# A decoder layer in fp32: convolution and later additions issued inside the next unit of products, whole results added up by one transfer, fewer operand sums by transfer, buffer halves paired by group

## The chip, the cores and the metric

The kernel runs on one core of a Trainium2 chip. The metric is device time in microseconds, from the first to the last instruction of the core and what lies around it. Three runs of the kernel before took 2989.66, 2991.01 and 2994.32 us; the median, 2991.01 us, is the time before. Engines are named as the profile names them: PE multiplies matrices, DVE works on vectors, ACT evaluates functions and copies with a scale, POOL issues transfers here (and does little else), SP issues loads.

## The reference

One decoder layer on 512 tokens with 2048 features, in fp32. The first half is a mixer (two kinds of attention, with a projection in and out); the change touches only where it stores some of its results. The second half is where most of the change lies:

```python
def conv_ffn(h, w_up, conv_w, conv_b, w_down):
    u = h @ w_up                                  # 512 x 2048 times 2048 x 11264
    S = u.shape[1]
    up = jnp.pad(u, ((0, 0), (CONV_WIDTH - 1, 0), (0, 0)))
    u = conv_b + sum(conv_w[i] * up[:, i:i + S] for i in range(CONV_WIDTH))
    a, b = jnp.split(u, 2, axis=-1)
    return (jax.nn.silu(a) * b) @ w_down          # 512 x 5632 times 5632 x 2048

def reference(x, c, positions, ...):
    ...
        h = rmsnorm(x, g_ffn[layer]) * (1 + sc2) + sh2
        x = x + (1 + gt2) * conv_ffn(h, w_up[layer], conv_w[layer], conv_b[layer], w_down[layer])
    return rmsnorm(x, g_final)
```

## The kernel before, in words

Features lie on the 128 partitions and the 512 tokens along the free axis. Each fp32 operand is split into a rounded high part and the rest: `parts` makes `wh` on ACT (L140) and `wl` on DVE (L142) of a weight chunk of 128x1024, and there are three buffers for each of the two. A product is then a few matmuls with high and low parts.

Most of the large products are done in **units** (`unit`). A unit computes two 128x512 results, `c1` and `c2`, from four quarters of a weight matrix (A11, A12, A21, A22, each 128x1024) with seven products instead of eight. In PE's order these are B11, T1, T2, B21, T3, B22 and T4. They take as weights a11; s = a21 + a22; s + a11; a12; a11 + a21; a12 + s; a22. Their outputs go to three banks, r1, r2 and r3. B21 adds onto r1 after B11 has been read from it, T3 and then T4 add onto r2 after what stands there was read, and B22 adds onto r3 after T1 was read. So PE waits for ACT's and DVE's readings of the banks as well as for its weights. Consecutive units take turns with two sets of banks, "acc" and "att".

In a **wide** unit the moving operand of six products has 512 columns: high and low part of the other factor side by side. Each bank then holds two 256-column partial results, which have to be summed, and part of these additions is done by transfers that add to their destination (`add`, L242, issued by POOL). Such a unit issues four of 128 KB: `l1` onto the left half of c1, `p5` onto the right half of c2, `u2` onto the right half of c1, and at the end `p1` onto the left half of c2. `l1` and `u2` are halves of a tile "sp", `p1` and `p5` are halves of a tile "ta". Two stages use wide units: 41 for `w_up` and 8 for `w_down1`. The units of `w_up` also make two of the weight sums by transfer (`by_dma`): s is a21 with a22 added from memory, and d = a21 + a11 is a second load of a21 with a11 added from memory.

After a unit of `w_up` comes `finish`: for each of the two results a causal convolution (`conv`: one pass of ACT, L1039, and two of DVE, L1040 and L1041), a Silu on ACT (L1046), a multiplication on DVE (L1048) and a store (L1049). The results of three further blocks, `ups`, come from a plain product ahead of the units and are finished beside the first three units. After a unit of `w_down1` each result is added to an earlier partial sum that a transfer loads (L1145, L1146), and stored (L1147).

Weights come through a ring of eight buffers "raw", loaded by SP in program order. Results and split operands lie in 31 tiles "F" of 128x1024; `slot` hands out halves of such a tile, two consecutive requests of the same group sharing one, and a tile comes free when both halves are done with.

The program is written as one sequence; a scheduler sets the order of each engine's instructions when it is built. Each engine then works through its own list strictly in order, and an instruction that waits holds up everything behind it on that engine. `behind(pins)` makes the scheduler issue what stands inside it only after the pinned instructions. `unit` has two such places: `between(0, ...)` after the copy of T1's result, and `between(1, ...)` after the copies of B21's result.

Of the kernel before, what the change touches and what calls it, by code (L numbers as in the profile page):

```python
# [35 lines left out]
NU = 3  # L36
# [39 lines left out]
def block_kernel(ctx: ExitStack, tc: tile.TileContext, A: dict, out: bass.AP):  # L76
# [151 lines left out]
    def unit(src, f, between=lambda *_: None, wide=False, by_dma=False):  # L228
# [27 lines left out]
        if by_dma:  # L256
            s = a21
            add(s, src[3])
        else:
            a22 = load(src[3], w)  # L260
        a12 = load(src[1], w)
        if by_dma:
            d = load(src[2], w)
            add(d, src[0])
            a22 = load(src[3], w)
        product(r1, parts(a11, w), "B11", True)
        e = t2k("ta", 2)
        p1, p5 = both(e)
# [5 lines left out]
        if not by_dma:  # L274
            s = t2k("raw", 8, w=w)
            last_v = tt(s, a21, a22, ALU.add)
# [6 lines left out]
        u2, l1 = both(e)  # L283
# [7 lines left out]
        if wide:  # L291
            last = act(l1, r1[:, HALF:], AF.Copy)
            add(c1[:, :HALF], l1)
# [7 lines left out]
        if wide:  # L301
            tt(c2[:, HALF:], r2[:, HALF:], c2[:, HALF:], ALU.add)
            add(c2[:, HALF:], p5)
        else:
            tt(c2[:, HALF:], c2[:, HALF:], p5, ALU.add)
        tt(a12, a12, s, ALU.add)  # L306
        product(r3, parts(a12, w), "B22", False)
        if wide:
            act(c1[:, HALF:], r3[:, :HALF], AF.Copy)
            tt(u2, r3[:, HALF:], u2, ALU.add)  # L310
            add(c1[:, HALF:], u2)
        else:
            tt(c1[:, HALF:], r3[:, :HALF], u2, ALU.add)
        product(r2, parts(a22, w), "T4", False)
        if wide:
            act(c2[:, :HALF], r2[:, :HALF], AF.Copy)
            tt(p1, r2[:, HALF:], p1, ALU.subtract)
            add(c2[:, :HALF], p1)
        else:
            tt(c2[:, :HALF], r2[:, :HALF], p1, ALU.subtract)  # L320
# [118 lines left out]
    def evac(ps, rows=slice(0, P)):  # L439
        o = slot()  # L440
        act(o[rows], ps[rows], AF.Copy)
        return o
# [232 lines left out]
    def fetch(src, rows=slice(0, P)):  # L675
        t = slot()
        save(t[rows], src[rows])
        return t
# [7 lines left out]
    def values(g, vs):  # L686
# [12 lines left out]
        for b in range(NQB):  # L699
            vs.append(evac(pv[b]))  # L700
# [11 lines left out]
    def indexer():  # L712
# [11 lines left out]
        bias.extend(slot()[:, : (b + 1) * P] for b in range(1, NQB))  # L724
# [65 lines left out]
    pairs = [[fetch(xd[2 * i]), fetch(xd[2 * i + 1])] for i in range(1)]  # L790
# [49 lines left out]
    def stick_4(hd, w, vs):  # L840
# [4 lines left out]
        ya[hd] = evac(o)  # L845
# [7 lines left out]
    va = [fetch(vd[b]) for b in range(NQB)]  # L853
    before = None
    def turned(hd):
        pair = [fetch(xd[16 + 2 * hd + i]) for i in range(2)]
        for t in pair:
            rope(t, [t], cosT, sinT, 64)
        return pair

    td = dram("td", KT)
    for hd in range(NH):
        state = stick_1(hd)
        if hd + 1 < NH:
            pairs.append([fetch(xd[2 * hd + 2]), fetch(xd[2 * hd + 3])])
        if before:
            stick_4(*before, va)
            if hd % 4 == 0:
                va = [fetch(vd[hd + b]) for b in range(NQB)]
        run(fill, 1 if hd < 4 else 2)  # L870
        if hd == NH - 1:
            cosT, sinT = (fetch(rope_d[0][:, i * S : (i + 1) * S]) for i in range(2))
            for i in range(4):
                ya[i] = fetch(yad[i])
# [51 lines left out]
    def sparse_4(hd, pT, vs, y):  # L926
# [5 lines left out]
        y.append(evac(o))  # L932

    def branch_a():
        w = prep(A["w_a"][0])
        g = fetch(xd[32])
        for j in range(KT):
            ahead = (prep(A["w_a"][j + 1]), fetch(xd[34 + 2 * j])) if j + 1 < KT else (None, None)
# [37 lines left out]
    for j in range(KT):  # L976
        t = t2k("w", 2)
        save(t, td[j])
        g = fetch(xd[33 + 2 * j])
# [314 lines left out]
```

## Time and profile before

| what | value |
|---|---|
| median of three runs | 2991.01 us |
| the profiled execution | 2988.76 us |
| its span, first to last instruction | 2986.8 us |
| PE busy in the span | 2814.4 us, 94% |
| DVE busy | 2343.7 us, 78% |
| ACT busy | 1420.4 us, 48% |
| POOL busy | 509.9 us, 17% |
| granted PE clock, mean | 0.982 |
| bytes moved by transfers | 598.41 MB, 200 GB/s |

A busy PE is not PE at its peak, because matmuls overlap; what counts is how long PE waits and how far apart matmuls start. Idle time of an engine that nothing waits for costs nothing. The stage of the `w_up` units runs from about 1528 to 2497 us, that of `w_down1` from about 2560 to 2722 us.

### The profile page before, as it was taken

The numbers are of one execution on the slowest core, as the hardware profiler recorded it, in microseconds if no ns is written. First come the engines' busy times: TensorE is split into PE (matmuls) and PEld (weight loads), VectorE is DVE, ScalarE is ACT, GpSimd is POOL, SyncE is SP. The second block draws the span as 40 slices with busy tenths as digits, with TensorE's granted clock in tenths as the row PEclk, the third lists the DMA queues.
The fourth block names the chain that finished last, engine by engine and source line by source line (L and its number), as shares of the span: only waits on it lengthen the run. The fifth ranks groups of instructions, "written<-read, shape, count | busy, mean of one in ns | idle before, by whom it ended". The sixth has DMA issues, their size and how long they took to land.

```text
span 2986.8 us, 45295 instructions
## 1 busy us (share of the span) xinstructions
PE 2814.4 (94%) x17174; PEld 2484.2 (83%) x17174; DVE 2343.7 (78%) x3448; ACT 1420.4 (48%) x2083; POOL 509.9 (17%) x727
## 2 busy tenths in 40 slices
PE   7999999999999999999998888889889899998998
PEld 6779999999987778899887777777777778887887
DVE  8979888888877998899877676766667777887555
ACT  5554544455546555344554444444444445544222
POOL 0000000100111211112212222222222221221111
PEclk9999999999999999999999999999999999999999
DMA  9954456555563668644467888777878786668754
GB/s 350 339 205 157 151 198 208 194 166 183 191 239 129 221 202 285 228 163 163 170 167 181 198 191 189 186 187 192 196 188 192 192 194 221 186 174 268 245 185 141
DMA packets 196186, 598.41 MB, mean 200 GB/s; under 512 B 24368, under 2 KB 53936, under 8 KB 195968
## 3 DMA queue, kind: packets, MB, share of 16 engines
q1 hardware_dynamic: 123312, 421.06, 42.7%
q0 software_dynamic: 72208, 174.07, 23.9%
q8 instruction: 135, 2.21, 0.3%
q14 instruction: 83, 0.68, 0.1%
q10 hardware_dynamic: 448, 0.39, 0.0%
HBM read 509.27 MB, written 60.46 MB: 191 GB/s over the span
## 4 chain that ended last, share of the span: by engine, by line
PE 19%; DMA 14%; DVE 10%; issue 5%; ACT 2%; POOL 1%; DVEq 0%; POOLq 0%; ACTq 0%; SPq 0%
DMA F<-sp 6%; DMA raw<-in_w_up 6%; DVE wl L142 4%; PE acc L251 2%; PE acc L152 2%; PE acc L153 2%; PE acc L154 2%; PE att L251 2%; DVE w L1040 2%; PE att L152 2%; PE att L154 2%; PE att L153 2%; DVE raw L306 1%; DMA F<-ta 1%; PE acc L252 1%
## 5 line engine op out<-in xcount | busy, mean ns | idle before, releaser
L140 ACT ACTIVATE wh<-raw 128x1024 fp32r<-128x1024 f32 (+2 forms) x787 | 814.0, 1041 | 1039.5 <-PE acc L153 200.9
L142 DVE TENSOR_TENSOR wl<-raw,wh 128x1024 fp32r<-128x1024 f32 (+2 forms) x787 | 949.0, 1214 | 199.5 <-ACT wh L140 192.5
L152 PE MATMUL acc<-F,wh 128*128 128x256 f32 (+2 forms) x1796 | 553.2, 311 | 19.6 <-ACT F L173 15.8
L154 PE MATMUL acc<-F,wl 128*128 128x256 f32 (+2 forms) x1796 | 555.5, 309 | 1.3 <-DVE wl L142 1.3
L153 PE MATMUL acc<-F,wh 128*128 128x256 f32 (+2 forms) x1796 | 555.8, 310 | 0.1
L152 PE MATMUL att<-F,wh 128*128 128x256 f32 (+1 forms) x1706 | 525.9, 310 | 9.8 <-ACT wh L140 9.3
L154 PE MATMUL att<-F,wl 128*128 128x256 f32 (+1 forms) x1706 | 526.1, 309 | 1.7 <-DVE wl L142 1.7
L153 PE MATMUL att<-F,wh 128*128 128x256 f32 (+1 forms) x1706 | 526.0, 308 | 0.2 <-DVE F L174 0.2
L251 PE MATMUL acc<-F,wh 128*128 128x512 f32 x1200 | 441.2, 409 | 39.0 <-ACT wh L140 36.4
L251 PE MATMUL att<-F,wh 128*128 128x512 f32 x1152 | 421.0, 407 | 34.9 <-ACT wh L140 32.6
L152 PEld LDWEIGHTS acc<-F,wh 128*128 128x128 f32 (+1 forms) x1796 | 341.9, 191 | 41.7 <-ACT F L173 17.8
L154 PEld LDWEIGHTS acc<-F,wl 128*128 128x128 f32 (+1 forms) x1796 | 342.6, 191 | 20.0 <-DVE wl L142 2.1
L153 PEld LDWEIGHTS acc<-F,wh 128*128 128x128 f32 (+1 forms) x1796 | 342.6, 191 | 19.9 <-DVE F L174 2.1
L252 PE MATMUL acc<-F,wl 128*128 128x256 f32 x1200 | 341.6, 287 | 16.4 <-DVE wl L142 16.2
L152 PEld LDWEIGHTS att<-F,wh 128*128 128x128 f32 x1706 | 326.1, 191 | 28.7 <-ACT wh L140 10.9
L252 PE MATMUL att<-F,wl 128*128 128x256 f32 x1152 | 326.4, 286 | 16.8 <-DVE wl L142 16.8
L154 PEld LDWEIGHTS att<-F,wl 128*128 128x128 f32 x1706 | 325.7, 191 | 18.5 <-DVE wl L142 3.1
L153 PEld LDWEIGHTS att<-F,wh 128*128 128x128 f32 x1706 | 326.2, 191 | 17.8 <-DVE F L174 2.3
L251 PEld LDWEIGHTS acc<-F,wh 128*128 128x128 f32 x1200 | 232.8, 194 | 99.9 <-ACT wh L140 46.1
L251 PEld LDWEIGHTS att<-F,wh 128*128 128x128 f32 x1152 | 221.7, 193 | 94.3 <-ACT wh L140 42.9
L340 DVE SCALAR_TENSOR_TENSOR raw<-raw,raw 128x1024 f32<-128x1024 f32 x186 | 226.0, 1225 | 64.9 <-DMA raw<-in_w_ada 64.9
L252 PEld LDWEIGHTS acc<-F,wl 128*128 128x128 f32 x1200 | 234.1, 195 | 23.7 <-DVE wl L142 22.2
(303 smaller groups left out, 3741.1 us busy)
## 6 DMA issues: line engine op xcount, KB each, us to landing
raw<-in_w_up SPq DMA_DIRECT2D x205, 512.0 KB, 5.0
raw<-in_w_ada SPq DMA_DIRECT2D x186, 512.0 KB, 4.8
raw<-in_w_x SPq DMA_DIRECT2D x128, 512.0 KB, 4.2
raw<-in_w_up POOLq DMA_DIRECT2D x82, 512.0 KB, 5.3
raw<-in_w_down SPq DMA_DIRECT2D x64, 512.0 KB, 4.4
xd<-F POOLq DMA_DIRECT2D x64, 256.0 KB, 2.7
F<-xd POOLq DMA_DIRECT2D x64, 256.0 KB, 4.6
raw<-in_w_o SPq DMA_DIRECT2D x32, 512.0 KB, 4.3
```

Source lines behind the costliest of these rows:

```text
L140: act(wh, raw, AF.Copy)
L142: tt(wl, raw, wh.bitcast(F32), ALU.subtract)
L152: mm(ps, ah, bh, start=first, stop=False, skip_group_check=not check)
L153: mm(ps, ah, bl, start=False, stop=False, skip_group_check=not check)
L154: mm(ps, al, bh, start=False, stop=last, skip_group_check=not check)
L251: mm(ps, ah, b, start=start, stop=False, skip_group_check=True)
L252: mm(ps[:, :HALF], al, b[:, :HALF], start=False, stop=stop, skip_group_check=True)
L306: tt(a12, a12, s, ALU.add)
L340: stt(raw, raw, 1.0, cb[half], ALU.mult, ALU.mult, accum_out=macc[:, t, half : half + 1])
L1040: stt(t[:, 1:], u[:, : S - 1], cw[:, j, 1:2], t[:, 1:], ALU.mult, ALU.add)
```

## The change

Four things are done.

1. In the units of `w_up`, the results are no longer finished after their unit. They go to a list, `ready`, and the next unit's `between` calls `finish` for them behind B21's copies (the three early `ups` share the first two units with them). In `w_down1`, the addition of the earlier partial sum (`add_first`) is moved in the same way: one result at each `between` of the next unit.
2. In wide units, two transfers of 256 KB add up a whole result each, c1 += e and c2 += p, at the end of their result, in place of four of 128 KB. The halves of e change places, so that it lies like c1.
3. In the units of `w_up`, s = a21 + a22 is made by DVE, of a loaded a22 and in place; only d = a21 + a11 is still made by transfer. a22 is loaded third instead of last.
4. Halves of "F" tiles are shared only by requests of the same group (q and k, values, gates, and so on).

```diff
@@ unit @@
         a11 = load(src[0], w)
         a21 = load(src[2], w)
-        if by_dma:
-            s = a21
-            add(s, src[3])
-        else:
-            a22 = load(src[3], w)
+        a22 = load(src[3], w)
         a12 = load(src[1], w)
         if by_dma:
             d = load(src[2], w)
             add(d, src[0])
-            a22 = load(src[3], w)
         product(r1, parts(a11, w), "B11", True)
-        e = t2k("ta", 2)
-        p1, p5 = both(e)
+        p = t2k("ta", 2)
+        p1, p5 = both(p)
...
-        if not by_dma:
-            s = t2k("raw", 8, w=w)
-            last_v = tt(s, a21, a22, ALU.add)
+        s = a21 if by_dma else t2k("raw", 8, w=w)
+        last_v = tt(s, a21, a22, ALU.add)
         product(r3, parts(s, w), "T1", True)
...
         e = t2k("sp", 2)
-        u2, l1 = both(e)
+        l1, u2 = both(e)
...
             last = act(l1, r1[:, HALF:], AF.Copy)
-            add(c1[:, :HALF], l1)
         between(1, last, last_v)
...
             tt(c2[:, HALF:], r2[:, HALF:], c2[:, HALF:], ALU.add)
-            add(c2[:, HALF:], p5)
...
             tt(u2, r3[:, HALF:], u2, ALU.add)
-            add(c1[:, HALF:], u2)
+            add(c1, e)
...
             tt(p1, r2[:, HALF:], p1, ALU.subtract)
-            add(c2[:, :HALF], p1)
+            add(c2, p)
@@ evac and fetch; thirteen callers name a group in the same way @@
-    def evac(ps, rows=slice(0, P)):
-        o = slot()
+    def evac(ps, rows=slice(0, P), group=""):
+        o = slot(group=group)
...
-            vs.append(evac(pv[b]))
+            vs.append(evac(pv[b], group="vb"))
...
-    va = [fetch(vd[b]) for b in range(NQB)]
+    va = [fetch(vd[b], group="va") for b in range(NQB)]
@@ the units of w_up @@
     ups = [evac(ps) for ps in ups]
+    ready = [(j, *ups[2 * j : 2 * j + 2]) for j in range(NU)]
+
+    def between(i, *pins):
+        if len(ready) > 1 - i:
+            with behind(*pins):
+                finish(*ready.pop(0))
+
+    finish(*ready.pop(0))
     for j in range(NU, NJ):
-        if j < 2 * NU:
-            finish(j - NU, *ups[2 * (j - NU) : 2 * (j - NU) + 2])
-        finish(j, *unit(A["w_up"][j - NU], f, wide=True, by_dma=True))
+        ready.append((j, *unit(A["w_up"][j - NU], f, between, wide=True, by_dma=True)))
+    finish(*ready.pop())
@@ the units of w_down1 @@
+    def add_first(j, o):
+        t = t2k("w", 2)
+        save(t, sumd[j])
+        tt(o, o, t, ALU.add)
+        save(sumd2[j], o)
+
+    def between(i, *pins):
+        if ready:
+            with behind(*pins):
+                add_first(*ready.pop(0))
+
     for u in range(KT // 2):
-        for i, o in enumerate(unit(A["w_down1"][u], f, wide=True)):
-            j = 2 * u + i
-            t = t2k("w", 2)
-            save(t, sumd[j])
-            tt(o, o, t, ALU.add)
-            save(sumd2[j], o)
+        ready += enumerate(unit(A["w_down1"][u], f, between, wide=True), 2 * u)
+    for r in ready:
+        add_first(*r)
```

How the scheduler's order moves is shown for three engines, each in the middle of the `w_up` stage, for one unit.

**ACT**, before, from the first convolution of the unit that has just ended (its results are in F, its weights were the one before) to the last weights of this unit:

```order
L1039 ACTIVATE w_19033<-F_18959,cw 128x512
L270 ACTIVATE ta_19079<-acc_19044 128x256
L140 ACTIVATE wh_19135<-raw_19052 128x1024
L1039 ACTIVATE w_19038<-F_18959,cw 128x512
L1046 ACTIVATE w_19033<-w_19033 128x512
L140 ACTIVATE wh_19159<-raw_19054 128x1024
L278 ACTIVATE ta_19079<-acc_19046 128x256
L140 ACTIVATE wh_19183<-raw_19052 128x1024
L140 ACTIVATE wh_19206<-raw_19057 128x1024
```

The same in the change; L265 here is L270 there, L1031 is L1039, L1038 is L1046:

```order
L265 ACTIVATE ta_21364<-acc_21330 128x256
L140 ACTIVATE wh_21421<-raw_21339 128x1024
L140 ACTIVATE wh_21455<-raw_21341 128x1024
L272 ACTIVATE ta_21364<-acc_21332 128x256
L140 ACTIVATE wh_21478<-raw_21339 128x1024
L140 ACTIVATE wh_21501<-raw_21337 128x1024
L284 ACTIVATE F_21441<-acc_21330 128x256
L286 ACTIVATE sp_21418<-acc_21330 128x256
L1031 ACTIVATE w_21444<-F_21247,cw 128x512
L1031 ACTIVATE w_21449<-F_21247,cw 128x512
L140 ACTIVATE wh_21538<-raw_21527 128x1024
L1038 ACTIVATE w_21444<-w_21444 128x512
```

The convolution of the unit before stood ahead of the reading of B11 and of the weights of B21, T3, B22 and T4. It now stands behind all of them and behind the copies of B21's result.

**DVE**, before, from the same convolution to the low parts of B22's weights; L306 makes a12 + s in place:

```order
L1040 SCALAR_TENSOR_TENSOR w_21385<-F_21311,cw,w_21385 128x511
L271 TENSOR_TENSOR ta_21431<-acc_21396,ta_21431 128x256
L1041 SCALAR_TENSOR_TENSOR w_21385<-F_21311,cw,w_21385 128x510
L142 TENSOR_TENSOR wl_21489<-raw_21404,wh_21487 128x1024
L1040 SCALAR_TENSOR_TENSOR w_21390<-F_21311,cw,w_21390 128x511
L142 TENSOR_TENSOR wl_21513<-raw_21406,wh_21511 128x1024
L1041 SCALAR_TENSOR_TENSOR w_21390<-F_21311,cw,w_21390 128x510
L306 TENSOR_TENSOR raw_21404<-raw_21404,raw_21401 128x1024
L1048 TENSOR_TENSOR w_21385<-w_21385,w_21390 128x512
L284 TENSOR_TENSOR sp_21484<-ta_21431,acc_21397 128x256
L286 TENSOR_TENSOR sp_21484<-sp_21484,acc_21397 128x256
L142 TENSOR_TENSOR wl_21537<-raw_21404,wh_21535 128x1024
```

In the change, two pieces of one unit. First the turn from one unit to the next: the unit's last subtraction (L309, of T4's result), s + a11 of the next (L274), the new a21 + a22 of the unit after it (L270), and the low parts of T2's weights:

```order
L309 TENSOR_TENSOR ta_21170<-att_21137,ta_21170 128x256
L274 TENSOR_TENSOR raw_21335<-raw_21335,raw_21333 128x1024
L270 TENSOR_TENSOR raw_21529<-raw_21529,raw_21531 128x1024
L142 TENSOR_TENSOR wl_21400<-raw_21335,wh_21398 128x1024
L266 TENSOR_TENSOR ta_21364<-acc_21330,ta_21364 128x256
```

Then the rest of that unit, from a12 + s (L298) to the convolution of the unit before it (L1032 and L1033, F_21247):

```order
L298 TENSOR_TENSOR raw_21339<-raw_21339,raw_21335 128x1024
L142 TENSOR_TENSOR wl_21457<-raw_21341,wh_21455 128x1024
L278 TENSOR_TENSOR sp_21418<-ta_21364,acc_21331 128x256
L280 TENSOR_TENSOR sp_21418<-sp_21418,acc_21331 128x256
L142 TENSOR_TENSOR wl_21480<-raw_21339,wh_21478 128x1024
L142 TENSOR_TENSOR wl_21503<-raw_21337,wh_21501 128x1024
L1032 SCALAR_TENSOR_TENSOR w_21444<-F_21247,cw,w_21444 128x511
L293 TENSOR_TENSOR F_21441<-acc_21331,ta_21364 128x256
L1033 SCALAR_TENSOR_TENSOR w_21444<-F_21247,cw,w_21444 128x510
L1032 SCALAR_TENSOR_TENSOR w_21449<-F_21247,cw,w_21449 128x511
L295 TENSOR_TENSOR F_21441<-acc_21331,F_21441 128x256
L1033 SCALAR_TENSOR_TENSOR w_21449<-F_21247,cw,w_21449 128x510
```

The convolution's passes have moved from among the weights of B21 and T3 to the readings of T3's result (L293, L295), which PE's T4 waits for. One addition of 128x1024 per unit is new on DVE.

**POOL**, before, one unit: the store of a convolution, two additions in the middle of the unit, the weight sum s of the unit after next, two additions at the end, the weight sum d:

```order
L1049 DMA yd_15108<-w_21189 128x512
L242 DMA F_21311<-sp_21288 128x256
L242 DMA F_21311<-ta_21235 128x256
L242 DMA raw_21597<-in_w_up 128x1024
L242 DMA F_21311<-sp_21288 128x256
L242 DMA F_21311<-ta_21235 128x256
L242 DMA raw_21602<-in_w_up 128x1024
```

The same in the change (F_21053's additions end one unit; raw_21341 is d of the unit after next, whose a11 is raw_21333):

```order
L242 DMA F_21053<-sp_21030 128x512
L242 DMA F_21053<-ta_20976 128x512
L242 DMA raw_21341<-in_w_up 128x1024
L1041 DMA yd_15109<-w_21250 128x512
L242 DMA F_21247<-sp_21224 128x512
L242 DMA F_21247<-ta_21170 128x512
```

Seven transfers a unit have become four, and both additions of a unit's results now stand at its end.

More of the change, by code (lines that the diff above doesn't have):

```diff
@@ L672, in block_kernel, with fetch @@
             save(xd[2 * u + i], o)
-    def fetch(src, rows=slice(0, P)):
-        t = slot()
+    def fetch(src, rows=slice(0, P), group=""):
+        t = slot(group=group)
         save(t[rows], src[rows])
@@ L723, in indexer @@
         nc.vector.tensor_copy(wi.rearrange("p b h -> p (b h)"), wps[:, : NQB * IDXH])
-        bias.extend(slot()[:, : (b + 1) * P] for b in range(1, NQB))
+        bias.extend(slot(group="bias")[:, : (b + 1) * P] for b in range(1, NQB))
         yield
@@ L789, in block_kernel @@
         exp_ln = nc.scalar.preload_act_table_set("natural_log_exp_and_others").ins
-    pairs = [[fetch(xd[2 * i]), fetch(xd[2 * i + 1])] for i in range(1)]
+    pairs = [[fetch(xd[2 * i + n], group="qk") for n in range(2)] for i in range(1)]
     def stick_1(hd):
@@ L844, in stick_4 @@
                skip_group_check=True)
-        ya[hd] = evac(o)
+        ya[hd] = evac(o, group="ya")
         if hd < 4:
@@ L852, in block_kernel @@
     fill = values(1, vb[1])
-    va = [fetch(vd[b]) for b in range(NQB)]
+    va = [fetch(vd[b], group="va") for b in range(NQB)]
     before = None
     def turned(hd):
-        pair = [fetch(xd[16 + 2 * hd + i]) for i in range(2)]
+        pair = [fetch(xd[16 + 2 * hd + i], group="qk") for i in range(2)]
         for t in pair:
@@ L864, in block_kernel @@
         if hd + 1 < NH:
-            pairs.append([fetch(xd[2 * hd + 2]), fetch(xd[2 * hd + 3])])
+            pairs.append([fetch(xd[2 * hd + n], group="qk") for n in (2, 3)])
         if before:
@@ L868, in block_kernel @@
             if hd % 4 == 0:
-                va = [fetch(vd[hd + b]) for b in range(NQB)]
+                va = [fetch(vd[hd + b], group="va") for b in range(NQB)]
         run(fill, 1 if hd < 4 else 2)
         if hd == NH - 1:
-            cosT, sinT = (fetch(rope_d[0][:, i * S : (i + 1) * S]) for i in range(2))
+            cosT, sinT = (fetch(rope_d[0][:, i * S : (i + 1) * S], group="rope") for i in range(2))
             for i in range(4):
-                ya[i] = fetch(yad[i])
+                ya[i] = fetch(yad[i], group="ya")
         later, last = stick_2(*state)
@@ L931, in sparse_4 @@
                    pT[b][:, kb * P : (kb + 1) * P], start=kb == 0, stop=kb == b)
-        y.append(evac(o))
+        y.append(evac(o, group="y"))
     def branch_a():
         w = prep(A["w_a"][0])
-        g = fetch(xd[32])
+        g = fetch(xd[32], group="gate")
         for j in range(KT):
-            ahead = (prep(A["w_a"][j + 1]), fetch(xd[34 + 2 * j])) if j + 1 < KT else (None, None)
+            ahead = (prep(A["w_a"][j + 1]), fetch(xd[34 + 2 * j], group="gate")) if j + 1 < KT else (None, None)
             ps = att()
@@ L978, in block_kernel @@
         save(t, td[j])
-        g = fetch(xd[33 + 2 * j])
+        g = fetch(xd[33 + 2 * j], group="gate")
         merged.append(g)
```

## The prediction

> **What bounds the kernel now.** I read the busy times by stage first, because the page's 94% for PE is an average over stages with different limits.
>
> ```profile
> core 0: us, PE busy (x) PEld busy (x) DVE busy (x) ACT busy (x) POOL busy (x), PEclk, DMA share, GB/s
> 250.00:880.00 630.00, 624.23 (x5145) 619.96 (x5144) 548.63 (x723) 308.76 (x402) 50.13 (x93) 1.00 0.56 186
> 880.00:1420.00 540.00, 530.09 (x2962) 444.11 (x2961) 479.88 (x845) 278.88 (x459) 96.86 (x165) 1.00 0.59 202
> 1528.00:2497.00 969.00, 864.98 (x4949) 746.02 (x4948) 684.19 (x879) 457.23 (x673) 235.81 (x286) 0.97 0.79 190
> 2560.00:2720.00 160.00, 156.93 (x947) 138.29 (x947) 134.69 (x166) 77.23 (x112) 43.28 (x60) 1.00 0.67 190
> ```
>
> Columns are the stretch, its length, the engines' busy time, the granted clock and the transfers' share. PE is idle 104 us in the `w_up` stage (969 - 865), 10 us in the attention stages and 3 us in `w_down1`. Only in `w_up` is the clock visibly below full (0.97). So the change has its room in the third row. Next, how long a unit takes there, by the start of the same instruction in the first and the last unit; then the same in `w_down1`:
>
> ```profile
> L316 ACT ACTIVATE F<-acc x21: 368/385/386, 1548.5 to 2492.1; 128x256 f32<-128x256 f32 x21
> ```
> ```profile
> L284 DVE TENSOR_TENSOR sp<-ta,att x4: 411/414/420, 2565.9 to 2688.5; 128x256 f32<-128x256 f32 x4
> L284 DVE TENSOR_TENSOR sp<-ta,acc x4: 411/414/416, 2586.3 to 2708.3; 128x256 f32<-128x256 f32 x4
> ```
> ```profile
> L271 DVE TENSOR_TENSOR ta<-acc,ta x2: 415/416/416, 2664.9 to 2704.4; 128x256 f32<-128x256 f32 x2
> ```
>
> "acc" is every other unit, so the first row spans 40 units: 943.6 / 40 = 23.59 us each. The `w_down1` units, with the same seven products, take (2708.3 - 2565.9) / 7 = 20.34 us on average and in their best stretch (third fence, two units) 19.75. What PE itself needs is read from the starts of its matmuls, the first of B11, of T1 and of T2:
>
> ```profile
> 1999.91 0.39 PE L251 MATMUL acc<-F,wh 128*128 128x512 f32 x1
> ...
> 2002.68 0.28 PE L152 MATMUL acc<-F,wh 128*128 128x256 f32 x1
> ...
> 2005.55 0.40 PE L251 MATMUL acc<-F,wh 128*128 128x512 f32 x1
> ```
>
> A wide product takes 2.77 us, T1 2.87, a unit 6 x 2.77 + 2.87 = 19.49. A `w_up` unit thus loses 23.59 - 19.49 = 4.10 us, 41 of them 168 us. For whom PE waits there, and for whom those wait:
>
> ```profile
> PE acc L251 <- ACT wh L140: 36.4, 23, 2.2
> PE att L251 <- ACT wh L140: 32.6, 25, 1.9
> PE att L252 <- DVE wl L142: 16.6, 17, 1.2
> PE acc L252 <- DVE wl L142: 15.3, 15, 1.3
> ```
> ```profile
> ACT w L1039 <- DMA F<-sp: 149.6, 41, 6.2
> DVE w L1040 <- ACT w L1039: 131.5, 44, 5.8
> ACT wh L140 <- DVE raw L306: 109.6, 39, 2.9
> ```
>
> PE waits for weights, 101 us in these rows, and no wait is longer than 2.2 us. The weights are late because ACT stands 149.6 / 41 = 3.65 us per unit at the convolution's first pass until the last addition onto c1 has landed. One unit on ACT shows what queues behind that:
>
> ```profile
> 2047.81 1.06 ACT L140 ACTIVATE wh<-raw 128x1024 fp32r<-128x1024 f32 x1 [0.60 <-DVE raw L280]
> 2052.72 0.82 ACT L1039 ACTIVATE w<-F,cw 128x512 f32<-128x512 f32 x1 [3.85 <-DMA F<-sp]
> 2053.44 0.36 ACT L270 ACTIVATE ta<-acc 128x256 f32<-128x256 f32 x1
> 2053.70 1.05 ACT L140 ACTIVATE wh<-raw 128x1024 fp32r<-128x1024 f32 x1
> ...
> 2055.94 1.04 ACT L140 ACTIVATE wh<-raw 128x1024 fp32r<-128x1024 f32 x1
> ...
> 2060.14 1.06 ACT L140 ACTIVATE wh<-raw 128x1024 fp32r<-128x1024 f32 x1 [2.88 <-DVE raw L306]
> ```
>
> Behind the wait stand the reading of B11's bank (2053.44), B21's weights (2053.70) and T3's (2055.94). DVE waits as long in its own copy of that queue, so a12 + s (L306) is late and B22's weights start only at 2060.14. PE runs dry from that.
>
> **The change, part by part.** *Convolution inside the next unit.* It now stands behind B21's copies. Let the next unit's B11 start at 0, with the floor's products: T1 at 2.77, T2 at 5.64, B21 8.41, T3 11.18, B22 13.95, T4 16.72, end 19.49. The additions are issued when B22 and T4 of the unit before have been read, some 0.3 us before and 1.2 us after 0. What a whole-tile addition of 256 KB takes isn't in the trace; the nearest rows are these:
>
> ```profile
> raw<-in_w_up SPq DMA_DIRECT2D x197, 512.0 KB, 5.0
> raw<-in_w_up POOLq DMA_DIRECT2D x79, 512.0 KB, 5.3
> yd<-w POOLq DMA_DIRECT2D x43, 256.0 KB, 4.7
> F<-sp POOLq DMA_DIRECT2D x82, 128.0 KB, 6.0
> ```
>
> The bounds are 4.7 (a plain store of that size) and 2 x 6.0 = 12.0 (two half additions one after the other). I take 7, near the last row, since the same kind of transfer grows little with size (512 KB of it land in 5.3). So c1 is whole at about 6.7 and c2 at about 8.2. ACT gets to the convolution after T4's weights, which wait for B21's buffer (11.2): about 12.9. The cover is 6 us for c1, and at 12.0 the additions would still land in time (11.7 and 13.2). If the cover were gone, the 3.65 us would come back at T4 instead of B21.
>
> *What DVE must do instead.* Starts on DVE when nothing is waited for:
>
> ```profile
> 2055.23 1.22 DVE L142 TENSOR_TENSOR wl<-raw,wh 128x1024 fp32r<-128x1024 f32 x1
> 2056.36 0.75 DVE L1040 SCALAR_TENSOR_TENSOR w<-F,cw,w 128x511 f32<-128x511 f32 x1
> 2057.03 1.22 DVE L142 TENSOR_TENSOR wl<-raw,wh 128x1024 fp32r<-128x1024 f32 x1
> 2058.16 0.75 DVE L1041 SCALAR_TENSOR_TENSOR w<-F,cw,w 128x510 f32<-128x510 f32 x1
> 2058.82 1.22 DVE L306 TENSOR_TENSOR raw<-raw,raw 128x1024 f32<-128x1024 f32 x1
> 2059.95 0.69 DVE L1048 TENSOR_TENSOR w<-w,w 128x512 f32<-128x512 f32 x1
> 2060.56 0.42 DVE L284 TENSOR_TENSOR sp<-ta,acc 128x256 f32<-128x256 f32 x1
> ```
>
> So 1.13 us for a 128x1024 pass, 0.67 for one of the convolution, 0.61 for the multiplication; a 256-column one I put at 0.35, under its 0.42. The new a21 + a22 adds 1.13 to the stage's 684.19 / 41 = 16.7 busy us per unit: 17.8 of at least 19.5. It fits, with the least room of all engines. I walked two places where DVE's order could hold PE. (a) At the turn of the unit T4's result can be read at 0.2. DVE finishes T1's low parts (0.4), subtracts (0.75), makes s + a11 from 1.1 to 2.2 and a21 + a22 to 3.4, while ACT makes T2's high part, and is through with T2's low parts at 4.8. T2 starts at 5.64: margin 0.8. (b) T4 adds onto r2, so it waits until L295 has read T3's result, there from 14.0. In front of L295 stand L293 and two convolution passes: T4's low parts end at 13.8, L1032 at 14.5, L293 at 14.9, two passes at 16.2, L295 at 16.55. T4 starts at 16.72: margin 0.2. The other weights have 1.1 us or more. So the unit comes down to the products or very near. For its length I take 19.9, the best `w_down1` stretch (19.75) and 0.15 for the narrow margin (b). Lower bound 19.49; for the upper bound see the rivals.
>
> *Loads.* In the ring of eight, a22 takes the buffer of d of two units before. DVE needs the next unit's a22 at 2.2. SP can send the next unit's a11, a21 and a22 in a burst once T4's weights of the unit before are made (13.8 there); with 5.0 to land, and about half a microsecond for the issues, a22 is there at about -0.2: margin 2.4. The load for d goes out when a12 + s has been made (7.2 of the previous unit), lands at 12.2, is added to by 12.2 + 0.9 + 5.3 = 18.4, about 1 us before the unit, and is wanted at 5.9: margin 7. One transfer of 512 KB per unit disappears, so the transfers' share stays at about 0.79 at the faster pace.
>
> *Clock.* The stage lost 0.03 x 969 = 29 us of PE cycles, part of the 168. Stages with little waiting (first, second and last row of the first fence) show 1.00, so I let it go with the waits. [...]
>
> *`w_down1`.* The addition moves behind later work. I take 19.75 for 20.34 in seven intervals: 4 us; bounds 0 and 6 (7 x 0.85).
>
> *Paired halves.* This moves rows in the attention stages alone. PE idles 10 us there, the most that could be won; I take 0, between -10 and +10.
>
> **Sum**, against the profiled execution, 2988.76 us (span 2986.8): 41 x (23.59 - 19.9) = 151, and 4, together 155, leave 2834. The median of the runs shown is 2.25 us above that execution: **2836 us**.
>
> **Rivals.** *A new wait takes back half* (12%). DVE stands at a21 + a22 for a late a22, or PE at T4 for L295, by some 1.6 us a unit. Three loads at once support the first (none is late in the trace before, where a22 came last and was used last), the margin of 0.2 the second. Units at 21.5 give 41 x 2.09 = 86, 2836 + 65 = 2901.
>
> *The clock stays low* (7%). If the half-speed stretches belong to the stage and not to its waits, 29 us stay: 2865. [...]
>
> *Slower: the weight sum d arrives late* (4%). ACT's high part for T3 now stands ahead of the reading of T1's bank, of B22's and of T4's weights, and d is now added to only in the unit before, where it had more than a unit's time. It decides when d lands more than 7 us late, and costs more than the 4.1 us won when it is over 11 us late; at 12 us the unit is 0.9 us longer than before, 2991 + 37 = 3028. Against it: no transfer in the stage's rows has a median over 6.0.
>
> *No change* (2%). The order shows the convolution moved. Still, if PE were held at the same places by DVE's late a12 + s for another reason, the moved work would only change who is named: 2991.
>
> **How the numbers follow.** Forecast 75%; the rivals 12, 7, 4 and 2%. All but the last two are faster. About 0.2%, 6 us, is what a measurement of this kernel can tell. Faster 0.94, same 0.02, slower 0.04. The forecast's own bounds are 41 x 0.41 = 17 us down for units at 19.49, 2 for `w_down1` and half of the 10 for the attention stages, some 2812. Upward the range takes in the clock's case and most of the way to the half-gain, which leaves out under 2 in 10: 2812 to 2885.
>
> **What would show it.** In the profile after, the wait of the convolution's ACT pass for F is gone or under 10 us in total; PE's waits for wh and wl in the stage fall from 101 us to under 25; the start of L308 (L316 before) comes every 19.5 to 20.3 us; PEclk in the stage is 0.99 or 1.00; DVE is 88 to 92% busy there. A wait of PE for F from L295, of DVE for `in_w_up`, or of ACT's wh for the POOL-issued d would show the rivals, and a clock still at 0.97 the second. The forecast is wrong if units stay above 21 us.

## The result

| | median of four runs | profiled execution | its span |
|---|---|---|---|
| before | 2990.34 us (2976.43 to 2994.32) | 2988.76 us | 2986.8 us |
| changed | 2851.89 us (2848.17 to 2854.29) | 2854.29 us | 2852.5 us |

The ratio is 0.9544, with an interval of 0.9511 to 0.9577: some 138 us less. The forecast was 2836, with a range of 2812 to 2885.

### The profile page after: what moved, and what is told of

The parts are those of the page before. It is cut to its first block, busy times and chain, and to the rows that moved or that the text cites. A ratio compares the mean times of both kernels' runs of the same rounds, so it can differ in the third digit from the quotient of the medians.

```text
span 2852.5 us, 44989 instructions
## 1 busy us (share of the span) xinstructions
PE 2773.4 (97%) x17174; PEld 2465.5 (86%) x17174; DVE 2392.0 (84%) x3489; ACT 1422.6 (50%) x2083; POOL 391.0 (14%) x588
## 4 chain that ended last, share of the span: by engine, by line
PE 77%; DVE 12%; DMA 5%; issue 3%; ACT 2%; POOL 0%; SPq 0%; DVEq 0%; ACTq 0%; POOLq 0%
PE att L251 9%; PE acc L251 9%; PE acc L152 7%; PE acc L154 7%; PE acc L153 7%; PE att L154 7%; PE att L152 7%; PE att L153 7%; PE att L252 5%; PE acc L252 4%; DVE wl L142 3%; DVE raw L332 2%; DMA raw<-in_w_va 1%; ACT wh L140 1%; DVE F L174 1%
## 5 line engine op out<-in xcount | busy, mean ns | idle before, releaser
L152 PE MATMUL acc<-F,wh 128*128 128x256 f32 (+2 forms) x1796 | 553.9, 311 | 19.6 <-ACT F L173 15.7
L152 PE MATMUL att<-F,wh 128*128 128x256 f32 (+1 forms) x1706 | 526.6, 310 | 8.4 <-ACT wh L140 7.9
L251 PE MATMUL acc<-F,wh 128*128 128x512 f32 x1200 | 427.5, 399 | 1.0 <-DVE F L295 0.7
L251 PE MATMUL att<-F,wh 128*128 128x512 f32 x1152 | 408.5, 398 | 3.4 <-ACT wh L140 3.4
L152 PEld LDWEIGHTS acc<-F,wh 128*128 128x128 f32 (+1 forms) x1796 | 342.1, 191 | 42.2 <-ACT F L173 17.9
L152 PEld LDWEIGHTS att<-F,wh 128*128 128x128 f32 x1706 | 326.4, 191 | 27.2 <-ACT wh L140 9.0
L251 PEld LDWEIGHTS acc<-F,wh 128*128 128x128 f32 x1200 | 226.1, 189 | 56.6 <-DVE sp L280 1.0
L252 PEld LDWEIGHTS acc<-F,wl 128*128 128x128 f32 x1200 | 227.4, 189 | 1.2 <-DVE wl L142 0.9
```

The costliest lines, as they stand in the source:

```text
L152: mm(ps, ah, bh, start=first, stop=False, skip_group_check=not check)
L251: mm(ps, ah, b, start=start, stop=False, skip_group_check=True)
L252: mm(ps[:, :HALF], al, b[:, :HALF], start=False, stop=stop, skip_group_check=True)
```

## The profile after

The first view is the one with which the prediction began: busy time of each engine by stage, with the granted clock and the transfers' share. The stages have moved, so the stretches of `w_up` and `w_down1` are others than before.

```profile
core 0: us, PE busy (x) PEld busy (x) DVE busy (x) ACT busy (x) POOL busy (x), PEclk, DMA share, GB/s
1532.00:1572.00 40.00, 35.00 (x202) 30.21 (x201) 31.16 (x40) 22.14 (x33) 4.56 (x7) 0.96 0.50 150
1572.00:2364.00 792.00, 790.03 (x4761) 698.99 (x4760) 699.18 (x877) 437.54 (x642) 127.38 (x159) 1.00 0.74 199
2364.00:2426.00 62.00, 59.79 (x258) 49.05 (x257) 45.85 (x84) 34.46 (x61) 9.78 (x18) 0.97 0.71 233
```

In the steady part of `w_up` (second stretch) PE is idle 2 us of 792, where it was idle 104 of 969; the clock is 1.00, and DVE is busy 699.18 / 792 = 88%. Just ahead of that part and behind it PE loses more: 5.0 of 40 us, and 2.2 of 62. For whom PE still waits more than 0.5 us in the whole of `w_up`:

```profile
PE att L251 <- ACT wh L140: 3.4, 1, 3.4
PE acc L154 <- DVE wl L142: 2.2, 1, 2.2
PE acc L153 <- DVE F L174: 1.9, 1, 1.9
PE acc L251 <- DVE F L295: 0.7, 1, 0.7
PE acc L252 <- DVE wl L142: 0.6, 1, 0.6
```

101 us of waiting for weights have become 6 (3.4 + 2.2 + 0.6), and every row is a single wait. ACT's longest waits for transfers, from the same stretch:

```profile
ACT w L1031 <- DMA yd<-w: 6.4, 1, 6.4
ACT w L1031 <- DMA F<-sp: 6.0, 1, 6.0
ACT w L1031 <- DMA F<-ta: 3.0, 1, 3.0
```

The 41 waits of 3.65 us are gone. What is left is one wait at the start of the stage (6.4, for a store) and two at its end (6.0 and 3.0, for the last unit's additions). Where the time came from is read from the starts of the same two instructions as before, ACT's copy of T4's result (L308, before L316) in the units of `w_up`, and the subtraction after T2 (L278, before L284) in those of `w_down1`:

```profile
L308 ACT ACTIVATE F<-acc x21: 367/385/386, 1560.0 to 2354.0; 128x256 f32<-128x256 f32 x21
```
```profile
L278 DVE TENSOR_TENSOR sp<-ta,att x4: 410/413/422, 2435.6 to 2554.6; 128x256 f32<-128x256 f32 x4
L278 DVE TENSOR_TENSOR sp<-ta,acc x4: 412/414/420, 2455.5 to 2573.4; 128x256 f32<-128x256 f32 x4
```

| stretch | before | after | gained |
|---|---|---|---|
| up to the first unit's T4 copy | 1548.5 us | 1560.0 us | -11.5 |
| 40 units of `w_up` | 943.6 | 794.0 | 149.6 |
| from the last T4 copy to `w_down1` | 2565.9 - 2492.1 = 73.8 | 2435.6 - 2354.0 = 81.6 | -7.8 |
| seven units of `w_down1` | 142.4 | 137.8 | 4.6 |
| the rest of the span | 278.5 | 279.1 | -0.6 |
| span | 2986.8 | 2852.5 | 134.3 |

A unit takes 794.0 / 40 = 19.85 us instead of 23.59. The stretch up to the first copy has two parts. PE's first product of the wide stage starts at 1528.4 before and at 1532.4 after (first row below of before, second of after), so 4.0 are lost ahead of it; the other 7.5 are lost in the first unit.

```profile
L251 PE MATMUL acc<-F,wh x96: 387/398/629, 1528.4 to 1600.0; 128*128 128x512 f32 x96
```
```profile
L251 PE MATMUL acc<-F,wh x96: 387/398/795, 1532.4 to 1598.9; 128*128 128x512 f32 x96
```

One unit in the middle, from the timelines of PE, POOL, ACT and DVE (start, duration, idle time before it and what ended it):

```profile
1976.18 0.40 PE L251 MATMUL acc<-F,wh 128*128 128x512 f32 x1
...
1979.01 0.28 PE L152 MATMUL acc<-F,wh 128*128 128x256 f32 x1
...
1981.89 0.40 PE L251 MATMUL acc<-F,wh 128*128 128x512 f32 x1
```
```profile
1976.17 0.90 POOL L242 DMA_DIRECT2D F<-sp  x1
1977.52 0.87 POOL L242 DMA_DIRECT2D F<-ta  x1 [0.45 <-DVE ta L309]
```
```profile
1989.16 1.51 ACT L1031 ACTIVATE w<-F,cw 128x512 f32<-128x512 f32 x2
```
```profile
1992.33 0.42 DVE L295 TENSOR_TENSOR F<-acc,F 128x256 f32<-128x256 f32 x1
```

B11 starts at 1976.18. The two additions are issued at -0.01 and 1.34, the convolution starts on ACT at 12.98 with no wait, and L295 has read T3's result at 16.57. The walk of the prediction had -0.3, 1.2, 12.9 and 16.55.

## The experiments

Each kernel was timed beside the kernel before on the same chip; ratios are against that. The theory: ACT, which works its list in order, stands for the landing of the last half addition, and that alone sets the unit's length. The rivals: the transfers bound the stage; the place of the convolution in the order matters in itself; or another part of the change gives the gain.

**The convolution's place alone.** From the kernel before; the additions, the sum s and the slots stay.

```diff
+    def between(i, *pins):
+        if len(ready) > 1 - i:
+            with behind(*pins):
+                finish(*ready.pop(0))
...
-        finish(j, *unit(A["w_up"][j - NU], f, wide=True, by_dma=True))
+        ready.append((j, *unit(A["w_up"][j - NU], f, between, wide=True, by_dma=True)))
```

> The kernel before, with only the convolution of w_up moved inside the next unit; four additions of 128 KB and both weight sums by transfer stay. Theory A (ACT's wait for the last addition to land is what made the weights late): nearly the whole gain comes back, a w_up unit of 19.8 to 20.8 us, 2850 to 2890 us in all; the transfers get tighter, since 0.79 x 23.6 = 18.6 us of their time per unit must fit, so up to 1 us per unit may stay. Rival B (the number and size of the transfers is what costs): at most a third of the gain, 2940 us or more. The convolution's ACT pass waits under 20 us in total for A, PE clock 1.00 in the stage.

Measured: 2846.33 us (2840.95 to 2847.41), ratio 0.9515 [0.9501, 0.9530]. The stage's row and the copy's starts:

```profile
1572.00:2360.00 788.00, 785.16 (x4731) 694.72 (x4730) 652.96 (x836) 436.23 (x639) 229.12 (x275) 1.00 0.90 223
```
```profile
L316 ACT ACTIVATE F<-acc x21: 367/384/385, 1553.5 to 2347.0; 128x256 f32<-128x256 f32 x21
```

Units of 793.5 / 40 = 19.84 us, as with the whole change. In the stretch of the row PE waits for nothing. The convolution's waits for landings fall from 149.6 us to 7.7 (4.5 and 3.2, both behind the last unit). The transfers move as much as before in less time, so their share rises to 0.90; a share of 0.79 was not a bound. This one edit holds the whole gain; the time lies 4 us under the expected range, and the units at its lower end.

**Whole additions alone.** From the kernel before, with one addition per result.

```diff
-            add(c1[:, :HALF], l1)
...
-            add(c2[:, HALF:], p5)
...
-            add(c1[:, HALF:], u2)
+            add(c1, e)
...
-            add(c2[:, :HALF], p1)
+            add(c2, p)
```

> The kernel before, with only the four half additions of a wide unit replaced by two whole ones; the convolution still follows its unit. Theory A: no gain, since c1's last addition is issued at the same moment and takes as long or longer to land; 2985 to 3030 us, ACT's wait for it 3.5 to 5 us per unit. Rival B: two transfers fewer per unit show as a gain, 2900 to 2960 us.

Measured: 2987.26 us, ratio 0.9994 [0.9983, 1.0005]: no change. The convolution's wait is still there, 143.4 / 41 = 3.50 us a unit:

```profile
ACT w L1037 <- DMA F<-sp: 143.4, 41, 6.3
```

Two transfers fewer per unit did not help here, with ACT still waiting these 3.50 us for the last one at the same place.

**The sum s on DVE alone.** From the kernel before; a22 is loaded earlier and added by DVE.

```diff
-        if by_dma:
-            s = a21
-            add(s, src[3])
-        else:
-            a22 = load(src[3], w)
+        a22 = load(src[3], w)
...
-            a22 = load(src[3], w)
...
-        if not by_dma:
-            s = t2k("raw", 8, w=w)
-            last_v = tt(s, a21, a22, ALU.add)
+        s = a21 if by_dma else t2k("raw", 8, w=w)
+        last_v = tt(s, a21, a22, ALU.add)
```

> The kernel before, with only s = a21 + a22 of the w_up units made by DVE. Theory A: no gain; DVE's queue gets 1.13 us longer per unit on the chain that makes weights late, so 2985 to 3035 us. Rival B: one accumulating transfer of 512 KB fewer per unit shows as a gain, 2920 to 2970 us.

Measured: 2992.34 us, ratio 1.0014 [0.9995, 1.0033]: no change.

```profile
ACT w L1033 <- DMA F<-sp: 150.1, 41, 7.7
DVE raw L270 <- DMA raw<-in_w_up: 90.3, 38, 4.6
```

The second row is the late a22 that the prediction had as a rival: DVE stands 2.4 us a unit for it. It shows no cost here, where ACT's wait comes anyway. In the changed kernel no such wait shows.

**The change with s by transfer.** The same edit the other way round, in the changed kernel.

```diff
-        a22 = load(src[3], w)
+        if by_dma:
+            s = a21
+            add(s, src[3])
+        else:
+            a22 = load(src[3], w)
...
+            a22 = load(src[3], w)
...
-        s = a21 if by_dma else t2k("raw", 8, w=w)
-        last_v = tt(s, a21, a22, ALU.add)
+        if not by_dma:
+            s = t2k("raw", 8, w=w)
+            last_v = tt(s, a21, a22, ALU.add)
```

> The changed kernel, with s = a21 + a22 of the w_up units made by transfer again (a22 loaded last). Theory A: DVE is the engine with the least room but not the bound, so giving it 1.13 us per unit back changes little: 2845 to 2865 us. Rival (DVE's order holds PE at T4, or a late a22 does): a unit below 19.7 us, 2835 us or less. Rival B (transfers are the bound): 2880 us or more.

Measured: 2851.13 us, ratio 0.9531 [0.9515, 0.9547], units of (2351.7 - 1557.8) / 40 = 19.85 us. DVE is busy 654 of 788 us and the transfers' share is 0.86; in the changed kernel it is 699 of 792 and 0.74. Neither is the bound, so it makes no difference which of the two carries s.

**Both weight sums on DVE.** The changed kernel, with d made by DVE too.

```diff
-        ready.append((j, *unit(A["w_up"][j - NU], f, between, wide=True, by_dma=True)))
+        ready.append((j, *unit(A["w_up"][j - NU], f, between, wide=True)))
```

> The changed kernel, with both weight sums of the w_up units made by DVE, so that no accumulating load and one load fewer remain per unit, and DVE has 1.13 us more, some 18.6 of 19.84 us. Theory: PE's products are the bound and DVE still fits: unit 19.8 to 20.0 us, within 8 us of the changed kernel. Rival (DVE is at its limit, the margin at T4 was 0.2 us): PE waits for L295 or for low parts, unit 20.3 us or more, 2870 us or more.

Measured: 2861.22 us, ratio 0.9577 [0.9556, 0.9597], 9 us above the changed kernel on the same chip (2852.51).

```profile
1572.00:2360.00 788.00, 777.92 (x4684) 685.85 (x4683) 723.35 (x898) 434.39 (x630) 90.80 (x118) 1.00 0.52 144
```
```profile
PE acc L251 <- DVE F L295: 10.1, 19, 0.5
```

One more pass of 1.13 us brings DVE to 723 / 788 = 92%, and PE waits 0.5 us in every other unit for L295. That is the margin (b) of the prediction, crossed at the place where it was thinnest. The time lies between the two that were expected. The pass is not the only difference: in those units DVE's list now has the multiplication ahead of L295, and PE's list has the first matmul of the next unit ahead of T4. The 40 units take 2361.3 - 1553.3 = 808.0 us, 14 more than with the change, and an earlier first copy (1553.3) gives some of it back.

**The changed kernel again, and without groups.** In the second, `slot` gets no group, so the halves pair as before.

```diff
-        o = slot(group=group)
+        o = slot()
...
-        t = slot(group=group)
+        t = slot()
...
-        bias.extend(slot(group="bias")[:, : (b + 1) * P] for b in range(1, NQB))
+        bias.extend(slot()[:, : (b + 1) * P] for b in range(1, NQB))
```

> The changed kernel again, on the chip of the three below, as their yardstick: 2846 to 2858 us; w_up units of 19.84 us, a first unit of about 27 us.

> The changed kernel without the groups for halves of F tiles (the group of c1 and c2 and of the split operands stays, as before the change). Theory: the groups neither win nor cost more than 6 us, so within 6 us of the changed kernel. Rival (the groups cost what the attention stages lost, or win there): 6 to 15 us to either side, and the difference stands between 880 and 1420 us.

Measured: 2852.51 us (ratio 0.9544 [0.9523, 0.9564]) and 2844.46 us (2844.11 to 2848.13; ratio 0.9522 [0.9503, 0.9541]). The kernel without groups is 8 us faster, and its first copy of T4's result shows where:

```profile
L308 ACT ACTIVATE F<-acc x21: 364/383/386, 1551.6 to 2347.2; 128x256 f32<-128x256 f32 x21
```

1551.6 against 1560.0 is 8.4 us, all ahead of that copy, and not between 880 and 1420 us, where it was expected. The 40 units behind it take 795.6 us against 794.0. One wait of the changed kernel, from the sparse attention stage, is in all six traces of kernels with groups and in none without:

```profile
PE att L154 <- DVE wl L142: 4.7, 1, 4.7
```

It explains little: all of PE's waits between 1015 and 1200 us add up to 6.0 us in the changed kernel and 5.2 without groups. That groups as such cost 8 us is not shown either. With s by transfer the first copy comes at 1557.8 with groups (above) and at 1558.2 without (further below), and those two kernels lie 5 us apart, on different chips. From PE's first product of the stage to that copy, the kernels with the convolution inside take 23.0 to 27.9 us with groups and 21.7 to 26.2 without. What sets the length of this first unit stays open.

**The product stored from F.** The changed kernel, with the gated result written over the convolution's input, so that the store reads F and the work buffer "w" is free at once.

```diff
-        tt(a, a, b, ALU.mult)
-        nc.gpsimd.dma_start(yd[j // 2][:, j % 2 * S : (j % 2 + 1) * S], a)
+        tt(ua, a, b, ALU.mult)
+        nc.gpsimd.dma_start(yd[j // 2][:, j % 2 * S : (j % 2 + 1) * S], ua)
```

> The changed kernel, with the product of the convolution written over its own input in F and stored from there, so that its two work buffers come free without the store's landing. Theory: the 7 us that the first unit of w_up loses are the second early finish waiting for a work buffer whose store has not landed; they go, 5 to 8 us faster than the changed kernel, first unit 20 to 22 us. Rival (the loss is the double load of ACT and DVE in that unit): the first unit stays above 24 us and the time within 2 us.

Measured: 2852.13 us, ratio 0.9541 [0.9521, 0.9561]: as the changed kernel, so the theory failed. In the first unit of that one ACT waits 6.4 us for the store that still reads "w"; here the same wait stands at the copy of B21's result, for the F tile:

```profile
ACT F L284 <- DMA yd<-F: 6.4, 1, 6.4
```

Another buffer does not end the wait, since the store itself lands late. In the changed kernel it is issued at 1545.14, 0.55 us behind a weight addition of 512 KB in the same queue, and ACT goes on at 1552.48; in the steady units a store lands in 2.4 us by its median. Where it loses that time stays open. The first unit is shorter here (1558.8 - 1535.3 = 23.5 us in place of 27.6), but it starts 2.9 us later, for a reason that was not found either.

**Additions on DVE, convolution left after the unit.** From the kernel before; the four half additions are done by DVE, and nothing is moved.

```diff
-            add(c1[:, :HALF], l1)
+            tt(c1[:, :HALF], c1[:, :HALF], l1, ALU.add)
...
-            add(c2[:, HALF:], p5)
+            tt(c2[:, HALF:], c2[:, HALF:], p5, ALU.add)
...
-            add(c1[:, HALF:], u2)
+            tt(c1[:, HALF:], c1[:, HALF:], u2, ALU.add)
...
-            add(c2[:, :HALF], p1)
+            tt(c2[:, :HALF], c2[:, :HALF], p1, ALU.add)
```

> The kernel before, with the four half additions of a wide unit made by DVE in place of transfers (some 1.4 us more on DVE per unit); the convolution still follows its unit and still stands ahead of the next unit's weights. Theory A (the wait for the landing alone makes the weights late): ACT's wait at the convolution falls from 3.65 us per unit to under 1, a w_up unit of 19.9 to 20.8 us, 2850 to 2890 us in all. Rival A2 (the place of the convolution is the trouble: its 2.1 us on ACT and 3.3 us on DVE ahead of the weights): units of 22 us or more, 2930 us or more.

Measured: 2838.05 us (2837.33 to 2840.07), ratio 0.9489 [0.9473, 0.9505]. This is the fastest kernel here, 14 us below the changed one and 12 under the expected range.

```profile
1572.00:2360.00 788.00, 785.09 (x4729) 695.26 (x4728) 701.26 (x1001) 433.15 (x641) 88.45 (x117) 1.00 0.73 197
```
```profile
L316 ACT ACTIVATE F<-acc x21: 384/385/387, 1550.4 to 2352.5; 128x256 f32<-128x256 f32 x21
```

In the row's stretch the convolution waits for a transfer only once, 3.2 us for a store, and never for a result. So it may stand after the unit, as long as it doesn't wait for a landing: that wait made the weights late. The 40 units take 802.1 us, 8 more than with the change; the second and the third take 24.2 and 24.6 us, and two finishes stand ahead of each. But the first copy comes 9.6 us earlier, and from the last copy to the end it takes 2836.3 - 2352.5 = 483.8 us instead of 498.5. Half of that, 7.3 us, lies ahead of `w_down1`, where no result has to land any more. Another 8.1 us lie behind `w_down1`: there PE's longest wait for a weight is 1.9 us instead of 7.3, and the reason was not found.

**The convolution at the first place.** The changed kernel, with the convolution behind T1's copy instead of B21's.

```diff
-        if len(ready) > 1 - i:
+        if ready:
```

> The changed kernel, with the convolution issued at the first place of the next unit, behind the copy of T1's result, about 7 us after the unit's start, in place of 13. In the changed kernel c1's addition is issued at the unit's start and c2's 1.3 us after it, and the whole-tile additions land in 3.4 and 5.5 us by their medians. Theory A: 7 us is just cover enough, unit 19.8 to 20.3 us, 2845 to 2875 us. Rival (the place behind B21 is needed, since landings spread or since DVE's passes now stand ahead of T3): unit 20.8 us or more, 2885 us or more.

Measured: 2957.72 us (2956.7 to 2959.85), ratio 0.9889 [0.9874, 0.9903], 106 us above the changed kernel. It is slow, but not because the additions land late. The first fence groups instructions by line (busy time, mean ns, idle time before them), the second has PE's waits:

```profile
L1031 ACT ACTIVATE w<-F,cw 128x512 f32<-128x512 f32 x68 | 52.0, 808 | 3.5 <-DMA F<-ta 3.4
L270 DVE TENSOR_TENSOR raw<-raw,raw 128x1024 f32<-128x1024 f32 x35 | 42.9, 1226 | 80.1 <-DMA raw<-in_w_up 80.0
```
```profile
PE att L251 <- DVE sp L280: 29.7, 17, 2.0
PE acc L251 <- DVE sp L280: 24.4, 17, 2.0
```

The convolution waits 3.4 us for landings in 34 units; so a cover of some 5 us was enough here, where the additions land in 3.3 and 4.6 us by their medians (in one unit c2's is issued at 1922.95, and ACT's two passes start at 1927.32, together 1.51 us long). Two things are different. DVE stands 80 / 35 = 2.3 us a unit for a22, because in this order a21 + a22 comes earlier in its list. And its four convolution passes now lie in front of the reading of T2's result (L278, L280), as the timeline of DVE shows:

```profile
1929.97 1.41 DVE L1032 SCALAR_TENSOR_TENSOR w<-F,cw,w 128x511 f32<-128x511 f32 x2
1931.30 1.40 DVE L1033 SCALAR_TENSOR_TENSOR w<-F,cw,w 128x510 f32<-128x510 f32 x2
1932.62 0.41 DVE L278 TENSOR_TENSOR sp<-ta,att 128x256 f32<-128x256 f32 x1
```

T3 adds onto that bank, so PE waits for it 1.6 us in every unit (54.1 / 34), and the clock of the stage is 0.97 again. The wait has come back at another place, with another owner. Which of the two causes has the larger part was not separated. In the chain of work that ended last they are links of one loop: the load of a22 (5.9 us) is issued when DVE has made the low parts behind L280, and a21 + a22, s + a11 and the four passes follow behind it on DVE.

**Without groups, and s by transfer.** Two edits from above together, on the changed kernel.

> The changed kernel without the groups of F halves and with s by transfer again, so that of the change the convolution inside the next unit, the later additions of w_down1 and the whole-result additions remain. If the costs found so far add up (groups 8 us, s on DVE 0 to 2 us): 2841 to 2846 us. If the groups' cost comes from how the order happens to fall and not from the groups as such: anything from 2840 to 2855.

Measured: 2846.46 us (2845.14 to 2849.93), ratio 0.9517 [0.9503, 0.9532]. That is half a microsecond above what adding up the costs gave. Nothing is gained over the kernel without groups (2844.46, on another chip).

**Additions on DVE and the convolution inside the next unit.** The edit of the first experiment and that of the fastest kernel together.

> Kernel before with both cures at once: the four half additions on VectorE (no transfer lands on a result) and the convolution issued inside the next unit. If the landing of the last addition was the whole trouble, its place gives nothing more once no transfer lands: units of 19.8 us, 2838 to 2848, within 10 us of the kernel with the additions on VectorE alone (2838). If the place had a worth of its own, the first units (23.9 and 24.9 us there) come near 19.8 too and the time falls below 2833. If VectorE, 701 us busy in 788, is too full for another order of its passes, the units alternate as with both weight sums on VectorE: 2850 to 2862.

Measured: 2870.49 us (2868.18 to 2871.39), ratio 0.9596 [0.9578, 0.9614]: 24 and 32 us above the two kernels that have one of the edits each. None of the three expected ranges holds it. The units don't alternate; all take (2385.8 - 1556.9) / 40 = 20.72 us.

```profile
PE acc L152 <- ACT wh L140: 16.7, 21, 0.8
PE att L152 <- ACT wh L140: 15.3, 19, 0.8
```
```profile
1945.19 0.63 ACT L1046 ACTIVATE w<-w 128x512 f32<-128x512 f32 x1 [0.77 <-DVE w L1041]
1945.96 1.06 ACT L140 ACTIVATE wh<-raw 128x1024 fp32r<-128x1024 f32 x1
```
```profile
1947.07 0.39 PE L152 MATMUL acc<-F,wh 128*128 128x256 f32 x1 [0.80 <-ACT wh L140]
1947.29 0.39 PE L251 MATMUL att<-F,wh 128*128 128x512 f32 x1
```

PE waits 0.8 us in each unit for T1's weights. It needs them early: in its list the first matmuls of the next unit's B11 and T1 (L152, bank "acc") stand ahead of T4 of this one (bank "att"), which they don't in the middle of the stage in either of the two kernels with one edit. ACT makes those weights behind the Silu of the convolution, and the Silu stands 0.77 us for DVE's pass L1041. So what is shown to cost the time is the order that the scheduler made of the two edits, and not DVE's load as such.

## Why the prediction was right, and where it was off

**What bounds the kernel: right.** ACT's wait for the landing was the cause of PE's waits for weights. Taking the landing out of its way, by moving the convolution or by dropping the transfers, brings the unit to 19.84 or near it; the other edits alone give nothing.

**The unit's length: right.** 19.9 was taken, 19.85 measured; 40 intervals gained 149.6 us against 147.6. The floor was too low: the products took 2.83 us (B11) and 2.88 (T1), not 2.77 and 2.87, so a unit needs 6 x 2.83 + 2.88 = 19.86, and at that pace nothing is left to win there. The 2.77 was no misreading: in the kernel before, 27 of the 41 B11 products of the stage took 2.77 or 2.78 us and 11 took 2.82 to 2.84; after, all 39 of the steady part take 2.83. Why the quicker pace is gone stays open. The 0.15 for the margin (b) made up for it by chance. With the longer products T4 starts at 1993.20, 17.02 after B11, so that margin was 0.45 instead of 0.2.

**The cover: right, with room.** The whole additions land in 3.4 and 5.5 us (below), both under the 7 taken, and the first under the lower bound of 4.7. The weight addition for d went the other way, 7.6 us in place of 5.3, inside its margin of 7. The transfers' share fell to 0.74, where 0.79 was expected.

**The clock: right.** It went with the waits, from 0.97 to 1.00 in the steady part.

**`w_down1`: right in size.** 4.6 us against 4. No run separates the moved addition from the whole additions there; with the additions on DVE and nothing moved, the seven units take 138.5 us, nearly as little as the 137.8 here.

**What was mis-sized is the edges, 21 us.** The sum had 155 us (151.3 + 4), the spans differ by 134.3. (The medians differ by 138.5, since the profiled execution was 1.6 us below its median before and 2.4 above it after.) That the time still fell into the range was in part luck: its upper end was set for the clock's case, and not for the edges. Three terms make up the 21 us. The first: "41 x (23.59 - 19.9)" let the first unit gain like the others. It lost 7.5 instead of gaining 3.7, and ACT waits 6.4 us there for a store, with three finishes within one unit's length and two work buffers:

```profile
1545.28 0.81 ACT L1031 ACTIVATE w<-F,cw 128x512 f32<-128x512 f32 x1
1552.48 0.81 ACT L1031 ACTIVATE w<-F,cw 128x512 f32<-128x512 f32 x1 [6.39 <-DMA yd<-w]
...
2360.37 0.81 ACT L1031 ACTIVATE w<-F,cw 128x512 f32<-128x512 f32 x1 [6.03 <-DMA F<-sp]
2364.20 0.81 ACT L1031 ACTIVATE w<-F,cw 128x512 f32<-128x512 f32 x1 [3.01 <-DMA F<-ta]
```

The second is in the last two rows: the last unit has no next unit to hide its landing. It waits for both results, where the kernel before waited 4.4 us for one, and the way to `w_down1` is 7.8 us longer. The prediction had no term for that. The third is "paired halves, I take 0": 4.0 us were lost ahead of `w_up`, within the bound of 10. That the groups did this is likely and not certain: PE's first product of the stage starts at 1530.3 to 1535.3 in the six traces with groups and at 1525.8 to 1532.4 in the eight without. Together 11.2 + 7.8 + 4.0 = 23.0; the steady units (2.0 more) and `w_down1` (0.6) give a little back, and 0.6 is lost in the rest of the span.

**The rivals.** A new wait by L295 or a late a22 did not come in the changed kernel (0.7 us and none), but both were near: one more DVE pass, with the order that came with it, brought the first, an earlier place in the list the second. A late d did not come. The clock did not stay low.

## What to carry to other kernels

ACT, which works its list in order, stood 3.65 us a unit for a transfer to land, and that held up what stood behind it, so that PE waited 101 us for weights. In such a case find the landing that is waited for, and either put other work between issue and use (some 12 us of it in the changed kernel, some 5 in the one with the convolution at the first place), or let an engine with room do the work without a transfer. Both cures gave the same steady state (units of 19.84 us with the convolution inside, and with the additions on DVE 19.8 at the stage's end, the copies at 2332.7 and 2352.5), but the first leaves the last unit of a stage with nothing to hide its landings behind (waits of 6.0 and 3.0 us), and it crowds the first (6.4 us), so count units at the edges by themselves. Two good edits need not add up (2870 us together, 2846 and 2838 alone): each changes the order of the lists, and the place of one instruction decides whom it makes late.

## What the runs showed of the hardware

How long an addition by transfer takes did not follow its size. The rows give size and median time from issue to landing, in the changed kernel:

```profile
F<-sp POOLq DMA_DIRECT2D x40, 256.0 KB, 3.4
F<-ta POOLq DMA_DIRECT2D x40, 256.0 KB, 5.5
```

With s by transfer, and so with one more 512 KB addition per unit from the same queue, the same two take longer:

```profile
F<-sp POOLq DMA_DIRECT2D x39, 256.0 KB, 5.8
F<-ta POOLq DMA_DIRECT2D x39, 256.0 KB, 7.2
```

Half the size took 6.0 us in the kernel before. That the neighbours in the queue are the reason is argued from these rows, not shown apart, and the 512 KB weight additions don't bear it out: they landed in 7.6 us in the changed kernel and in 6.0 with s by transfer.

The granted clock of the stage was below 0.99 where PE's repeated waits reached 2 us. With waits of up to 2.2 us (before) or 2.0 us (convolution at the first place) the stage's clock was 0.97, with up to 2.1 us (s on DVE alone) 0.98; with 0.8 us in every unit (the last experiment) or none it was 1.00. Read in stretches of 2 us, the 0.97 of the kernel before is 18 short dips between 1528 and 2496 us, down to between 0.50 and 0.56 (0.50 from 2018 to 2020 us), with a clock of 1.00 between them: the half-speed stretches of the prediction. Each comes with a stretch in or just ahead of it in which PE is busy 1.5 us or less; but not every such stretch has one (from 2084 to 2086 PE is busy 0.33 us, and the clock stays at 1.00). The changed kernel has two dips, at 1554 and 2366 us, and none in the steady part. Which waits bring a dip was not shown.
